# Modulation weights on buffers and a queue of their own, a second norm with its affine ahead of the transposes, and three split-weight buffers

## The chip, the cores and the metric

The kernel runs on one core of a Trainium2 chip. The metric is the device time of one execution in microseconds (us). PE is TensorE (matmuls), DVE is VectorE, ACT is ScalarE, POOL is GpSimd; SP is the engine whose queue issues transfers. Names like L98 are line numbers of the program; after the change lines move by a few, and both numbers are given where it matters.

## What is computed

One layer of a diffusion block for 512 latent tokens with 256 context tokens ahead of them, width 1024, in float32:

```
sh1, sc1, ga1, sh2, sc2, ga2 = split(silu(c) @ w_mod + b_mod, 6)
hl = rmsnorm(x) * (1 + sc1) + sh1          # the context likewise, with c_ctx
p  = hl @ w_in                             # u, gate, q, k, v, output gate, scan gates, two branch gates
A  = silu(layernorm(dwconv(u * sigmoid(gate)))) @ w_conv_out            # y_conv
h  = bidirectional mLSTM(q, k, v), 4 heads of 512                       # context first, then latents
B  = (headnorm(h) * sigmoid(output gate)) @ w_m_out                     # y_m
x  = x + ga1 * ((sigmoid(gA) * A + sigmoid(gB) * B) @ w_out)            # x1
x  = x + ga2 * (relu((rmsnorm(x) * (1 + sc2) + sh2) @ w1) ** 2 @ w2)    # FFN, 4096 wide
out = rmsnorm(x)
```

The six modulation vectors are the columns of w_mod. The first two (sh1, sc1) are needed at once; the other four (ga1, sh2, sc2, ga2: channels 2 to 5 below) only after the mixer, and only for the latent tokens.

## The kernel before

All products are made in full precision from three passes of a faster matmul: each operand is split into a high part and a low part (the rest), and `mm3` (L101 to L104) adds high x high, high x low and low x high into one PSUM bank of 512 columns.

**Weights.** `wpiece` (L88) brings one piece of 512 KB (128 x 1024): a raw buffer (three of them, `wraw`), a transfer on SP's queue (L94), for w_out a multiplication by ga1 on DVE (L96), the high part by a cast on ACT (L97), the low part by a subtraction on DVE (L98). High and low parts go round in four buffers each. Activations are split the same way by `split` (L107, L108).

**Stages.** In order: the input's norm and modulation with the first feature tiles (0 to 60 us); the four heads of the mLSTM with the convolution's branch interleaved (to about 780); the end of the last head (its attention times v, `po`; its norm, L560 to L562; its transposes `th`) and the last five tiles of the branch gates (`pab`) to about 833; y_conv (w_conv_out, `pc`); y_m (w_m_out, `pym`); x1 (w_out, `pwo`, all eight PSUM banks open at once); the second norm; the FFN. In the first head the scan's gate recursions (L265 to L307) lie on DVE, beside the short convolutions (L334) and the wide one (L374).

**The late modulation.** `mod(ch, j)` (L643) fetches one 512 KB piece of w_mod's transposed columns (`wmt`, L645) and multiplies it on DVE by silu(c), spread over the partitions in `cB`, summing along the row (L646). There are 32 such pieces, four channels of eight. Their raw buffers are those of the weights, three for both, and their transfers go through SP's queue between the weights' (one also carries `hraw`, the mixer's output read back, L687). They are called from a list of small jobs (`queue`, `pump`) between the products of the gates, of y_conv and of y_m.

**The second norm.** For each of four tiles of 128 tokens, the last w_out products (the pieces from NP1 = 4 on) are added, then the residual (L783), the mean of squares on ACT, and the reciprocal root on POOL (L81, L82). Then ACT scales by it (L796), PE transposes 128 x 128 blocks (L799), and the affine with (1 + sc2) and sh2, which are per partition after the transpose, is done on the way out of PSUM: per block one operation on ACT (L805, the high part) and two on DVE (L807, L809, the low part).

**What sets the order.** The program is written engine-free; a scheduler orders each engine's instructions, and every engine and the SP queue then run their own list strictly in order. A tile from a pool of n buffers has to wait for the reader of the tile n before it.

Of the kernel before, what the change touches and what calls it, by code (L numbers as in the profile page):

```python
# [8 lines left out]
F32 = mybir.dt.float32  # L9
# [15 lines left out]
NS = 6                      # feature tiles computed while the input's norm comes in  # L25
NX = 3                      # and these while the context's comes in
# [7 lines left out]
# columns of the packed per-partition constants  # L34
# [13 lines left out]
def block(ctx, tc, a, out):  # L48
# [9 lines left out]
    # ------------------------------------------------------------ constants  # L58
# [25 lines left out]
    # ------------------------------------------------- weights in two parts  # L84
# [56 lines left out]
    with ExitStack() as hs:  # L141
# [3 lines left out]
        # ================================================ adaLN of the input  # L145
# [88 lines left out]
        # the context's part of the input, a tile between products  # L234
# [12 lines left out]
        # ============================================ heads of the mixer, GLU  # L247
# [133 lines left out]
        # statistics of the LayerNorm, about the mean of the first channels  # L381
# [188 lines left out]
        # first head: what needs only latent tokens goes first  # L570
# [34 lines left out]
    # ============================ branch gates, both branches, output, FFN  # L605
    with ExitStack() as fs:
        # over the heads' pools that are done first
        ma = fs.enter_context(tc.tile_pool(name="ma", bufs=7))
# [5 lines left out]
        def m4(shape, dt, nm, early=False):  # L614
            return (ma if early else mp).tile(shape, dt, tag="m", name=nm, bufs=7 if early else 9)
# [15 lines left out]
        cv = []  # L631
        for j in range(KT):
            if j % 2 == 0:
                c_ = m4([P, 2, T], F32, "cv", True)
            nc.sync.dma_start(out=c_[:, j % 2, :], in_=cdr[j])
            cv.append(c_[:, j % 2, :])

        # the other modulation columns (latent only)
# [4 lines left out]
        def mod(ch, j):  # L643
            raw = wraw("wmt")
            nc.sync.dma_start(out=raw, in_=a["wmt"][ch, j])  # L645
            nc.vector.scalar_tensor_tensor(out=raw, in0=raw, scalar=1.0, in1=cB, op0=ALU.mult, op1=ALU.mult,  # L646
                                           accum_out=modc[:, ch, j:j + 1])
# [33 lines left out]
        # the mixer's output in the transposed layout, read back in two parts  # L681
        hm_ = []

        def hmload(k):
            t_ = m4([P, 2, T], F32R, "hmT", k < 4) if k < KT else h6([P, 2, T], F32R, "hmT")
            raw = wraw("hraw")
            nc.sync.dma_start(out=raw[:, :T], in_=hd[k])  # L687
            split(t_[:, 0, :], t_[:, 1, :], raw[:, :T])
            hm_.append(t_)
# [6 lines left out]
        def row(ch, nm):  # L696
            r_ = m1p.tile([P, D], F32, tag="r2", name=nm)
            pr = bank("pr")
            nc.tensor.transpose(pr[0:KT, 0:P], modc[:, ch, :], ident)
            t_ = t2("rowt", P)  # L700
            nc.scalar.copy(out=t_[0:KT, :], in_=pr[0:KT, 0:P])
            rd = dr.tile([KT, P], F32, name=f"rowd{ch}")
# [4 lines left out]
        # y_conv, then y_m  # L707
# [7 lines left out]
        ga1 = row(2, "ga1")  # L715
        yT = []
        ws = []
        for j in range(KT):
            pc = bank("pym")
            for s in range(2):  # L720
                w = wpiece(a["wmo"][j, s], (KT, P))
                for k in range(KT):
                    kk = 8 * s + k
                    mm3(pc, (w[0][:, k, :], w[1][:, k, :]), (hm_[kk][:, 0, :], hm_[kk][:, 1, :]), kk == 0, kk == 15)
            if j == KT - 1:
# [4 lines left out]
            yt = m4([P, 2, T], F32R, "yT", j < 3)  # L730
            split(yt[:, 0, :], yt[:, 1, :], y_)
            yT.append(yt)
            pump(3)
        nc.vector.tensor_scalar(out=affc, in0=modc[:, 4, :], scalar1=1.0, scalar2=None, op0=ALU.add)
        nc.vector.tensor_tensor(out=affc, in0=affc, in1=ccol(O_G2, KT), op=ALU.mult)
# [20 lines left out]
        pump(99)  # L756
# [13 lines left out]
        h2T = [m4([P, 2, T], F32R, "h2T", k < 4) for k in range(KT)]  # L770
        for t in range(NT):
# [19 lines left out]
            xhs, pts = [], []  # L791
            for hf in range(2):
                pt = bank_a("pt2")
                pts.append(pt)
                xh = t2("xh")
                nc.scalar.activation(out=xh, in_=x1[t][:, hf * 512:(hf + 1) * 512], func=AF.Copy, scale=sq[:, 3:4])  # L796
# [187 lines left out]
```

## Time and profile before

| | |
|---|---|
| Time, median of 3 runs | 1386.22 us (1385.11 to 1386.37) |
| The profiled execution: span | 1384.5 us, that is 1.7 below the median |
| Input's norm, 0 to 60 us | PE busy 45.94 |
| First head, 110 to 230 | PE busy 114.61 of 120 |
| 230 to 742 | PE busy 512 of 512 |
| End of the last head and gates, 742 to 831 | PE busy 83.67 of 89 |
| y_conv and y_m, 831 to 963.6 | PE busy 132.6 of 132.6 |
| x1 and second norm, 963.6 to 1022 | PE busy 48.74 of 58.4 |
| FFN, 1022 to 1360 | PE busy 335.43 of 338 |

The profile lists for each engine its busy time; the waits name the instruction that waited, what ended the wait, and total, count and longest. In a timeline row stand the start, the duration, the engine, the line, the operation, what it writes and reads, and in square brackets the idle time just before it with what ended that. In a row of the windows stand, after the stretch and its length, the busy time and instructions of PE, PE's weight load, DVE, ACT and POOL, then the clock that TensorE was granted (1.00 is full), the busy share of the DMA engines, and GB/s.

### The profile page before, as it was taken

Reading aid. Unit: us, or ns where it says so; the run is one execution under the profiler, and the core shown is the slowest. Engines: PE = TensorE matmul, PEld = TensorE weight load, DVE = VectorE, ACT = ScalarE, POOL = GpSimd, SP = SyncE. Lnnn points to the kernel's source line nnn. Section 1 sums busy time; section 2 is a strip of 40 time slices with the busy share of each in tenths; the row PEclk is TensorE's granted clock in tenths of the full one; section 3 lists DMA queues with packets and bytes.
Section 4 is the critical chain, followed back from the end, with each engine's and each line's share of the span. In section 5 each row is a group of like instructions: output and inputs, shape, how many; then the busy total and the mean of one; then the engine's idle time right before and its main releaser. Section 6 shows DMA issues by size and latency. Waiting matters only on the chain.

```text
span 1384.5 us, 18697 instructions
## 1 busy us (share of the span) xinstructions
PE 1339.5 (97%) x7224; PEld 1155.2 (83%) x7224; DVE 951.5 (69%) x1532; ACT 608.3 (44%) x970; POOL 55.3 (4%) x199
## 2 busy tenths in 40 slices
PE   6999999999999999999999899999789999999997
PEld 4788889888998889988899778888678888888886
DVE  6799988489574895849995564666676554545454
ACT  4547554346443464434634373222376323433232
POOL 1000100000000000000000000000010000000001
PEclk9999999999999999999999999999899999999999
DMA  8783233223322233222324475776723223432211
GB/s 317 267 327 97 87 102 111 62 66 98 117 79 63 75 93 112 80 62 76 101 87 143 154 235 168 245 235 191 229 90 122 92 69 99 122 107 92 63 60 61
DMA packets 64604, 174.89 MB, mean 126 GB/s; under 512 B 6514, under 2 KB 18946, under 8 KB 64516
## 3 DMA queue, kind: packets, MB, share of 16 engines
q1 hardware_dynamic: 64516, 173.71, 39.4%
q8 instruction: 56, 0.92, 0.3%
q14 instruction: 32, 0.26, 0.1%
HBM read 161.68 MB, written 12.00 MB: 125 GB/s over the span
## 4 chain that ended last, share of the span: by engine, by line
PE 73%; DMA 10%; DVE 9%; ACT 4%; issue 3%; POOL 1%; SPq 0%; POOLq 0%; ACTq 0%; DVEq 0%
PE pf L103 8%; PE pf L102 8%; PE pf L104 8%; DMA wmt<-in_wmt 4%; PE pv L102 2%; PE pv L104 2%; PE pv L103 2%; PE pg L104 2%; PE pg L102 2%; PE pg L103 2%; PE pq L104 2%; PE pq L102 2%; PE pq L103 2%; DVE wlo L98 2%; PE p L104 2%
## 5 line engine op out<-in xcount | busy, mean ns | idle before, releaser
L97 ACT CAST whi<-wraw 128x1024 fp32r<-128x1024 f32 (+1 forms) x159 | 164.9, 1039 | 218.2 <-PE pf L103 43.7
L98 DVE TENSOR_TENSOR wlo<-wraw,whi 128x1024 fp32r<-128x1024 f32 (+1 forms) x159 | 191.8, 1208 | 91.6 <-ACT whi L97 90.8
L374 DVE SCALAR_TENSOR_TENSOR ca<-up,col,ca 128x512 f32<-128x512 f32 x240 | 179.5, 748 | 4.7 <-ACT ca L372 0.9
L334 DVE SCALAR_TENSOR_TENSOR cacc<-craw,col,cacc 128x512 f32<-128x512 f32 (+1 forms) x128 | 110.9, 881 | 0.1
L102 PE MATMUL pv<-whi,hT 128*128 128x256 f32 x384 | 109.3, 285 | 0.0
L104 PE MATMUL pv<-whi,hT 128*128 128x256 f32 x384 | 108.6, 283 | 0.0
L103 PE MATMUL pv<-wlo,hT 128*128 128x256 f32 x384 | 108.6, 283 | 0.0
L102 PE MATMUL pf<-w2h,fT 128*128 128x512 f32 x256 | 99.6, 389 | 0.0
L103 PE MATMUL pf<-w2l,fT 128*128 128x512 f32 x256 | 99.6, 389 | 0.0
L104 PE MATMUL pf<-w2h,fT 128*128 128x512 f32 x256 | 99.6, 389 | 0.0
L858 ACT CAST w2h<-w2raw 128x1024 fp32r<-128x1024 f32 x32 | 32.2, 1050 | 133.8 <-PE pf L104 111.5
L878 DVE TENSOR_TENSOR x<-pf,x 128x512 f32<-128x512 f32 x64 | 44.1, 689 | 63.8 <-PE pf L104 63.8
L102 PE MATMUL pf<-h2T,whi 128*128 128x512 f32 x224 | 87.1, 389 | 0.0
L103 PE MATMUL pf<-h2T,whi 128*128 128x512 f32 x224 | 87.1, 389 | 0.0
L104 PE MATMUL pf<-h2T,wlo 128*128 128x512 f32 x224 | 87.1, 389 | 0.0
L103 PE MATMUL p<-wlo,hT 128*128 128x256 f32 x256 | 73.2, 286 | 3.3 <-DVE wlo L98 3.3
L103 PEld LDWEIGHTS pv<-wlo,hT 128*128 128x128 f32 x384 | 73.7, 192 | 0.2 <-issue 0.2
L102 PEld LDWEIGHTS pv<-whi,hT 128*128 128x128 f32 x384 | 73.7, 192 | 0.2 <-DVE up L356 0.2
L104 PEld LDWEIGHTS pv<-whi,hT 128*128 128x128 f32 x384 | 73.7, 192 | 0.0
L102 PE MATMUL p<-whi,hT 128*128 128x256 f32 x256 | 73.0, 285 | 0.0
L104 PE MATMUL p<-whi,hT 128*128 128x256 f32 x256 | 73.0, 285 | 0.0
L856 DVE TENSOR_TENSOR w2raw<-w2raw,ga 128x1024 f32<-128x1024 f32 x32 | 39.0, 1225 | 47.9 <-DMA w2raw<-in_w 46.7
(350 smaller groups left out, 3463.7 us busy)
## 6 DMA issues: line engine op xcount, KB each, us to landing
wm<-in_wmt SPq DMA_DIRECT2D x32, 512.0 KB, 5.7
wraw<-in_wqk SPq DMA_DIRECT2D x32, 512.0 KB, 3.6
wmt<-in_wmt SPq DMA_DIRECT2D x32, 512.0 KB, 4.2
wraw<-in_w SPq DMA_DIRECT2D x32, 512.0 KB, 4.6
w2raw<-in_w SPq DMA_DIRECT2D x32, 512.0 KB, 3.5
wraw<-in_wglu SPq DMA_DIRECT2D x16, 512.0 KB, 4.4
wraw<-in_wp SPq DMA_DIRECT2D x16, 512.0 KB, 3.5
wraw<-in_wv SPq DMA_DIRECT2D x16, 512.0 KB, 3.6
```

Of the source, the lines that this page charges most:

```text
L97: nc.scalar.copy(out=hi[:, s], in_=raw[:, s])
L98: nc.vector.tensor_tensor(out=lo[:, s], in0=raw[:, s], in1=hi[:, s].bitcast(F32), op=ALU.subtract)
L102: mm(dst, lhsT=l[0], rhs=r[0], start=start, stop=False)
L103: mm(dst, lhsT=l[0], rhs=r[1], start=False, stop=False)
L104: mm(dst, lhsT=l[1], rhs=r[0], start=False, stop=stop)
L334: nc.vector.scalar_tensor_tensor(out=acc[:, :n], in0=raw[:, d:d + n], scalar=ccol(wc + d), in1=acc[:, :n], op0=ALU.mult, op1=ALU.add)
L374: nc.vector.scalar_tensor_tensor(out=accv, in0=up[:, :, d:d + 64], scalar=w_, in1=accv, op0=ALU.mult, op1=ALU.add)
L856: nc.vector.tensor_tensor(out=raw, in0=raw, in1=ga2, op=ALU.mult)
L858: nc.scalar.copy(out=hi, in_=raw)
L878: nc.vector.tensor_tensor(out=x1[t][:, nn], in0=pf, in1=x1[t][:, nn], op=ALU.add)
```

## The change

1. **Late modulation.** The 32 pieces get two buffers of their own ("wm"), and their transfers are issued by POOL (L651) instead of SP. `mod()` multiplies the piece that came longest ago (L658) and then fetches the next but one; two are fetched where the code stands. In program order one `mod()` stands after each tile of the branch gates, after each product of y_conv and after each half of y_m.
2. **Second norm.** (1 + sc2) times the norm's gain, and sh2, are transposed, written to DRAM and read back spread over all partitions (`aff2`, `sh2`). DVE applies reciprocal root and aff2 in one operation (L812), adds sh2 (L814), then PE transposes (L817), and one `split` per half tile (128 x 4 x 128) makes the high and low part.
3. **Buffers.** High and low parts of weights: three buffers each, not four. The convolved branch `cv`, the first half of the read-back mixer output and the norm's output `h2T` share one tile of 32 KB per partition ("big"); `hraw` gets buffers of its own pool. NP1 is 5 instead of 4.

```diff
-    wp = ctx.enter_context(tc.tile_pool(name="wp", bufs=4))
+    wp = ctx.enter_context(tc.tile_pool(name="wp", bufs=3))
...
-        def mod(ch, j):
-            raw = wraw("wmt")
-            nc.sync.dma_start(out=raw, in_=a["wmt"][ch, j])
+        mods = deque((ch, j) for ch in (2, 3, 4, 5) for j in range(KT))
+        mraw = deque()
+
+        def modfetch():
+            if mods:
+                ch, j = mods.popleft()
+                raw = wp.tile([P, D], F32, tag="wm", name="wmt", bufs=2)
+                nc.gpsimd.dma_start(out=raw, in_=a["wmt"][ch, j])
+                mraw.append((ch, j, raw))
+
+        def mod():
+            if not mraw:
+                return
+            ch, j, raw = mraw.popleft()
             nc.vector.scalar_tensor_tensor(out=raw, in0=raw, scalar=1.0, in1=cB, op0=ALU.mult, op1=ALU.mult,
                                            accum_out=modc[:, ch, j:j + 1])
...
+            modfetch()
+        modfetch()
+        modfetch()
...
-        for j in range(KT):
-            queue.append(lambda j=j: mod(2, j))
         for i in range(NS + NX + 2, 16):
             ab_tile(i)
-            pump(2)
-        pump(8)
+            mod()
...
-            raw = wraw("hraw")
-            nc.sync.dma_start(out=raw[:, :T], in_=hd[k])
+            raw = t2("hraw")
+            nc.sync.dma_start(out=raw, in_=hd[k])
...
-        for ch in (3, 4, 5):
-            for j in range(KT):
-                queue.append(lambda ch=ch, j=j: mod(ch, j))
...
+        aff2 = row(affc, h6([P, D], F32, "aff2"))
+        sh2 = row(modc[:, 3, :], h6([P, D], F32, "sh2"))
         po = [(bank_a if i < 4 else bank)("pwo") for i in range(8)]
-        NP1 = 4
+        NP1 = 5
...
-                nc.scalar.activation(out=xh, in_=x1[t][:, hf * 512:(hf + 1) * 512], func=AF.Copy, scale=sq[:, 3:4])
+                nc.vector.scalar_tensor_tensor(out=xh, in0=x1[t][:, hh], scalar=sq[:, 3:4], in1=aff2[:, hh],
+                                               op0=ALU.mult, op1=ALU.mult)
+                nc.vector.tensor_tensor(out=xh, in0=xh, in1=sh2[:, hh], op=ALU.add)
...
-                nc.scalar.activation(out=h2T[kk][:, 0, tt], in_=ps_, func=AF.Identity,
-                                     scale=affc[:, kk:kk + 1], bias=modc[:, 3, kk:kk + 1])
-                nc.vector.tensor_scalar(out=xh[:, ks], in0=ps_, scalar1=affc[:, kk:kk + 1],
-                                        scalar2=modc[:, 3, kk:kk + 1], op0=ALU.mult, op1=ALU.add)
-                nc.vector.tensor_tensor(out=h2T[kk][:, 1, tt], in0=xh[:, ks], in1=h2T[kk][:, 0, tt].bitcast(F32),
-                                        op=ALU.subtract)
+                ptv = pt.rearrange("p (k t) -> p k t", k=4)
+                kk = slice(4 * hf, 4 * hf + 4)
+                split(h2T[:, 0, kk, tt], h2T[:, 1, kk, tt], ptv)
```

What the scheduler makes of it, at four places. POOL's list from the last head's masks (L489) to its norm (L77, L78 are the reciprocal root of one token tile), before:

```order
L489 AFFINE_SELECT E1_7135<-E1_7135 128x128
L77 TENSOR_SCALAR sq_7560<-sq_7560 128x1
L78 TENSOR_TENSOR sq_7560<-sq_7560,nhalf_75 128x1
L77 TENSOR_SCALAR sq_7585<-sq_7585 128x1
L78 TENSOR_TENSOR sq_7585<-sq_7585,nhalf_75 128x1
L77 TENSOR_SCALAR sq_7621<-sq_7621 128x1
```

and after, from the last two of the sixteen fetches that now stand between the masks and the first reciprocal root:

```order
L651 DMA wmt_8408<-in_wmt 128x1024
L651 DMA wmt_8443<-in_wmt 128x1024
L77 TENSOR_SCALAR sq_7560<-sq_7560 128x1
L78 TENSOR_TENSOR sq_7560<-sq_7560,nhalf_75 128x1
L77 TENSOR_SCALAR sq_7585<-sq_7585 128x1
L78 TENSOR_TENSOR sq_7585<-sq_7585,nhalf_75 128x1
L651 DMA wmt_8481<-in_wmt 128x1024
L77 TENSOR_SCALAR sq_7621<-sq_7621 128x1
L651 DMA wmt_8515<-in_wmt 128x1024
```

Each of these fetches waits for the DVE multiplication two pieces before it, and the norm's operations stand behind them.

DVE's list around the reciprocal for the convolution's LayerNorm (L410) and the mixer's output (`hm`, L562), before:

```order
L646 SCALAR_TENSOR_TENSOR wmt_7925,modc_79<-wmt_7925,cB_7722 128x1024
L649 TENSOR_TENSOR modc_79<-modc_79,col_66 128x8
L98 TENSOR_TENSOR wlo_7854<-wraw_7852,whi_7853 128x1024
L108 TENSOR_TENSOR vlo_7178<-pv_7500,vhi_7177 128x256
L98 TENSOR_TENSOR wlo_7892<-wraw_7890,whi_7891 128x1024
L407 SCALAR_TENSOR_TENSOR lns2_536<-ps2_7528,sq_7532 128x512
L408 TENSOR_SCALAR lns2_536<-lns2_536 128x512
L410 RECIPROCAL lns2_536<-lns2_536 128x512
L562 SCALAR_TENSOR_TENSOR hm_7559<-po_7540,sq_7560,sg_6592 128x512
```

and after:

```order
L658 SCALAR_TENSOR_TENSOR wmt_8283,modc_79<-wmt_8283,cB_7719 128x1024
L98 TENSOR_TENSOR wlo_7849<-wraw_7847,whi_7848 128x1024
L407 SCALAR_TENSOR_TENSOR lns2_536<-ps2_7528,sq_7532 128x512
L658 SCALAR_TENSOR_TENSOR wmt_8328,modc_79<-wmt_8328,cB_7719 128x1024
L408 TENSOR_SCALAR lns2_536<-lns2_536 128x512
L658 SCALAR_TENSOR_TENSOR wmt_8370,modc_79<-wmt_8370,cB_7719 128x1024
L661 TENSOR_TENSOR modc_79<-modc_79,col_66 128x8
L410 RECIPROCAL lns2_536<-lns2_536 128x512
L562 SCALAR_TENSOR_TENSOR hm_7559<-po_7540,sq_7560,sg_6592 128x512
```

The piece wmt_8370 is the sixteenth (the second channel's last), where before the eighth (wmt_7925) was the last ahead of the reciprocal. After the hm operations, six more pieces stand ahead of the convolution's LayerNorm (cv).

DVE's list in the first head, at the low part of the fourth k tile's weights (wlo_1371), before:

```order
L271 SCALAR_TENSOR_TENSOR L_1123<-Gs_1112 64x768
L98 TENSOR_TENSOR wlo_1371<-wraw_1369,whi_1370 128x1024
L374 SCALAR_TENSOR_TENSOR ca_620<-up_537,col_66,ca_620 128x512 x3
L274 SCALAR_TENSOR_TENSOR L_1123<-Gs_1112,L_1123 64x768
L374 SCALAR_TENSOR_TENSOR ca_620<-up_537,col_66,ca_620 128x512
```

and after, where another piece (wlo_1299) stands in that place and wlo_1371 comes after the scans (L285) and the k tiles' convolutions:

```order
L299 TENSOR_TENSOR Z_1145<-Fr_1130,Mx_1132 32x512
...
L334 SCALAR_TENSOR_TENSOR cacc_1160<-craw_1159,col_66,cacc_1160 128x770
L334 SCALAR_TENSOR_TENSOR cacc_1232<-craw_1231,col_66,cacc_1232 128x770
L98 TENSOR_TENSOR wlo_1371<-wraw_1369,whi_1370 128x1024
L307 COPY zm_81<-pz_1441 128x512
L98 TENSOR_TENSOR wlo_1463<-wraw_1461,whi_1462 128x1024
```

In the x1 stage, what stands on DVE ahead of the product that frees the eighth bank (sig15 from pym), before:

```order
L646 SCALAR_TENSOR_TENSOR wmt_8942,modc_79<-wmt_8942,cB_7722 128x1024
L108 TENSOR_TENSOR yT_8844<-sig14_7763,yT_8844 128x512
L649 TENSOR_TENSOR modc_79<-modc_79,col_66 128x8
L96 TENSOR_TENSOR wraw_9012<-wraw_9012,ga1_8321 128x1024
L96 TENSOR_TENSOR wraw_9043<-wraw_9043,ga1_8321 128x1024
L98 TENSOR_TENSOR wlo_9014<-wraw_9012,whi_9013 128x1024
L96 TENSOR_TENSOR wraw_9074<-wraw_9074,ga1_8321 128x1024
L728 TENSOR_TENSOR sig15_7764<-pym_8856,sig15_7764 128x512
```

and after:

```order
L108 TENSOR_TENSOR yT_8838<-sig14_7764,yT_8838 128x512
L98 TENSOR_TENSOR wlo_8919<-wraw_8917,whi_8918 128x1024
L96 TENSOR_TENSOR wraw_9043<-wraw_9043,ga1_8330 128x1024
L742 TENSOR_TENSOR sig15_7765<-pym_8846,sig15_7765 128x512
L743 TENSOR_TENSOR sig15_7765<-sig15_7765,sig7_7757 128x512
```

The last multiplication of a modulation piece (before: wmt_8942) no longer stands here, and of the three scalings of w_out pieces one is left ahead of the product.

More of the change, by code (lines that the diff above doesn't have):

```diff
@@ L612, in block, with big, m4 @@
         m3p = fs.enter_context(tc.tile_pool(name="m3p", bufs=1))
-        def m4(shape, dt, nm, early=False):
-            return (ma if early else mp).tile(shape, dt, tag="m", name=nm, bufs=7 if early else 9)
+        def big(shape, dt, nm):
+            return ma.tile(shape, dt, tag="big", name=nm)
+        def m4(shape, dt, nm):
+            return mp.tile(shape, dt, tag="m", name=nm, bufs=8)
         def s2(nm, dt=F32):
@@ L630, in block @@
             lnr.append(r_)
-        cv = []
+        cvb = big([P, KT, T], F32, "cv")
+        cv = [cvb[:, j, :] for j in range(KT)]
         for j in range(KT):
[L633 to L636, printed above, removed]
+            nc.sync.dma_start(out=cv[j], in_=cdr[j])
         cB = m3p.tile([P, D], F32, tag="r1", name="cB")
@@ L684, in hmload, with row @@
         def hmload(k):
-            t_ = m4([P, 2, T], F32R, "hmT", k < 4) if k < KT else h6([P, 2, T], F32R, "hmT")
-            raw = wraw("hraw")
-            nc.sync.dma_start(out=raw[:, :T], in_=hd[k])
-            split(t_[:, 0, :], t_[:, 1, :], raw[:, :T])
-            hm_.append(t_)
+            if k == 0:
+                hb = big([P, KT, 2, T], F32R, "hmT")
+                hm_.extend(hb[:, i, :, :] for i in range(KT))
+            if k >= KT:
+                hm_.append(h6([P, 2, T], F32R, "hmT"))
+            raw = t2("hraw")
+            nc.sync.dma_start(out=raw, in_=hd[k])
+            split(hm_[k][:, 0, :], hm_[k][:, 1, :], raw)
         for k in range(16):
             queue.append(lambda k=k: hmload(k))
-        for ch in (3, 4, 5):
-            for j in range(KT):
-                queue.append(lambda ch=ch, j=j: mod(ch, j))
-        def row(ch, nm):
-            r_ = m1p.tile([P, D], F32, tag="r2", name=nm)
+        def row(src, r_):
             pr = bank("pr")
-            nc.tensor.transpose(pr[0:KT, 0:P], modc[:, ch, :], ident)
+            nc.tensor.transpose(pr[0:KT, 0:P], src, ident)
             t_ = t2("rowt", P)
             nc.scalar.copy(out=t_[0:KT, :], in_=pr[0:KT, 0:P])
-            rd = dr.tile([KT, P], F32, name=f"rowd{ch}")
+            rd = dr.tile([KT, P], F32, name="rowd")
             nc.sync.dma_start(out=rd, in_=t_[0:KT, :])
@@ L714, in block @@
             pump(2)
-        ga1 = row(2, "ga1")
+            mod()
+        ga1 = row(modc[:, 2, :], m1p.tile([P, D], F32, tag="r2", name="ga1"))
         yT = []
@@ L724, in block @@
                     mm3(pc, (w[0][:, k, :], w[1][:, k, :]), (hm_[kk][:, 0, :], hm_[kk][:, 1, :]), kk == 0, kk == 15)
+                if s == 0:
+                    mod()
             if j == KT - 1:
@@ L755, in block @@
                             k == 0, False)
-        pump(99)
+        while mraw:
+            mod()
         def w1first(i):
@@ L769, in block @@
         w1 = [w1first(i) for i in range(4)]
-        h2T = [m4([P, 2, T], F32R, "h2T", k < 4) for k in range(KT)]
+        h2T = big([P, 2, KT, T], F32R, "h2T")
         for t in range(NT):
@@ L790, in block @@
             rstd2(sq)
-            xhs, pts = [], []
             for hf in range(2):
+                hh = slice(hf * 512, (hf + 1) * 512)
+                xh = t2("xh")
+                nc.vector.scalar_tensor_tensor(out=xh, in0=x1[t][:, hh], scalar=sq[:, 3:4], in1=aff2[:, hh],
+                                               op0=ALU.mult, op1=ALU.mult)
+                nc.vector.tensor_tensor(out=xh, in0=xh, in1=sh2[:, hh], op=ALU.add)
                 pt = bank_a("pt2")
-                pts.append(pt)
-                xh = t2("xh")
-                nc.scalar.activation(out=xh, in_=x1[t][:, hf * 512:(hf + 1) * 512], func=AF.Copy, scale=sq[:, 3:4])
                 for k in range(4):
-                    kk = 4 * hf + k
                     nc.tensor.transpose(pt[:, k * P:(k + 1) * P], xh[:, k * P:(k + 1) * P], ident)
-                xhs.append(xh)
-            for kk in range(KT):
-                ks = slice((kk % 4) * P, (kk % 4 + 1) * P)
-                ps_ = pts[kk // 4][:, ks]
-                xh = xhs[kk // 4]
-                nc.scalar.activation(out=h2T[kk][:, 0, tt], in_=ps_, func=AF.Identity,
-                                     scale=affc[:, kk:kk + 1], bias=modc[:, 3, kk:kk + 1])
-                nc.vector.tensor_scalar(out=xh[:, ks], in0=ps_, scalar1=affc[:, kk:kk + 1],
-                                        scalar2=modc[:, 3, kk:kk + 1], op0=ALU.mult, op1=ALU.add)
-                nc.vector.tensor_tensor(out=h2T[kk][:, 1, tt], in0=xh[:, ks], in1=h2T[kk][:, 0, tt].bitcast(F32),
-                                        op=ALU.subtract)
+                ptv = pt.rearrange("p (k t) -> p k t", k=4)
+                kk = slice(4 * hf, 4 * hf + 4)
+                split(h2T[:, 0, kk, tt], h2T[:, 1, kk, tt], ptv)
         NG = 8
-        ga2 = row(5, "ga2")
+        ga2 = row(modc[:, 5, :], m1p.tile([P, D], F32, tag="r2", name="ga2"))
         fg = m3p.tile([P, D], F32, tag="r1", name="fg")
@@ L845, in ff1 @@
                 nc.scalar.activation(out=rl, in_=rl, func=AF.Square)
-                ft = h6([P, 2, T], F32R, "fT") if g % 2 == 0 else m4([P, 2, T], F32R, "fT", i < 3)
+                ft = h6([P, 2, T], F32R, "fT") if g % 2 == 0 else m4([P, 2, T], F32R, "fT")
                 split(ft[:, 0, :], ft[:, 1, :], rl)
```

17 lines of the change are left out of this document (9 added, 8 removed).

## The prediction

> **What bounds the kernel now.** I read the page's engine shares and its DMA issues first, then the waits of PE (TensorE's matmuls), then windows where PE is not full, then the timeline there.
>
> ```profile
> PE 1339.5 (97%) x7224; PEld 1155.2 (83%) x7224; DVE 951.5 (69%) x1532; ACT 608.3 (44%) x970; POOL 55.3 (4%) x199
> ...
> q1 hardware_dynamic: 64516, 173.71, 39.4%
> ...
> wm<-in_wmt SPq DMA_DIRECT2D x32, 512.0 KB, 5.7
> ...
> wmt<-in_wmt SPq DMA_DIRECT2D x32, 512.0 KB, 4.2
> ...
> w2raw<-in_w SPq DMA_DIRECT2D x32, 512.0 KB, 3.5
> ```
>
> PE is busy 97% of the span of 1384.5 us, so 45 us at most can come from filling its gaps; the matmuls stay as they are. A modulation column's 512 KB takes 4.2 us from issue to landing (median), and all of them go through SP's hardware queue: the page has no row of a transfer that POOL issues.
>
> ```profile
> PE pwo L102 <- DVE sig L728: 8.6, 1, 8.6
> PE pt L207 <- DVE xt L181: 7.4, 4, 3.5
> PE th L548 <- DVE hm L562: 3.7, 2, 1.9
> PE pt L799 <- ACT xh L796: 3.7, 4, 2.4
> ...
> PE p L103 <- DVE wlo L98: 3.3, 1, 3.3
> ```
>
> The columns are total us, times, longest. Two of these waits are what the change reaches for: one of 8.6 us where the x1 product opens its eighth bank, and four of 3.7 us together ahead of the second norm's transposes. The other three lie in stages that the change touches sideways: the startup (pt L207), the first head (p L103), the last head's end (th).
>
> **Part 1, the wait at x1 goes.** DVE, SP and PE around it:
>
> ```profile
> 967.89 1.22 DVE L646 SCALAR_TENSOR_TENSOR wmt<-wmt,cB 128x1024 f32<-128x1024 f32 x1
> ...
> 969.72 1.22 DVE L96 TENSOR_TENSOR wraw<-wraw,ga 128x1024 f32<-128x1024 f32 x1
> 971.88 1.22 DVE L96 TENSOR_TENSOR wraw<-wraw,ga 128x1024 f32<-128x1024 f32 x1 [0.94 <-DMA wraw<-in_wo]
> ...
> 975.20 1.23 DVE L96 TENSOR_TENSOR wraw<-wraw,ga 128x1024 f32<-128x1024 f32 x1 [0.96 <-DMA wraw<-in_wo]
> 976.34 0.69 DVE L728 TENSOR_TENSOR sig<-pym,sig 128x512 f32<-128x512 f32 x1
> ```
> ```profile
> 957.31 5.26 SPq L645 DMA_DIRECT2D wmt<-in_wmt  x3
> 965.67 3.81 SPq L94 DMA_DIRECT2D wraw<-in_wo  x3
> ```
> ```profile
> 977.08 0.80 PE L102 MATMUL pwo<-whi,yT 128*128 128x512 f32 x1 [8.57 <-DVE sig L728]
> 977.67 0.63 PE L103 MATMUL pwo<-wlo,yT 128*128 128x512 f32 x1
> 978.10 0.63 PE L104 MATMUL pwo<-whi,yT 128*128 128x512 f32 x1
> ...
> 981.48 0.39 PE L103 MATMUL pwo<-wlo,yT 128*128 128x512 f32 x1
> 981.71 0.39 PE L104 MATMUL pwo<-whi,yT 128*128 128x512 f32 x1
> ```
> ```profile
> 970.00:980.00 10.00, 2.92 (x7) 2.37 (x8) 7.56 (x8) 3.75 (x4) 0.00 (x0) 0.56 0.95 340
> 980.00:990.00 10.00, 10.00 (x43) 8.22 (x42) 5.62 (x5) 1.05 (x1) 0.00 (x0) 0.93 0.51 168
> ```
>
> The last three modulation columns hold SP's queue until 965.67, so three w_out pieces are issued late; DVE, in order, stands on their scaling (L96) before it reaches L728, which frees the bank. After the stall the granted clock is 0.56 and then 0.93 (the third column from the right), and some ten matmuls come 0.43 us apart instead of 0.23: about 2.0 us more. In the new order all columns are multiplied before y_m, and L742 (the old L728) has a single scaling of an early piece ahead of it. So -8.6 - 2.0 = **-10.6 us**. What is late next is the transfer of the w_out pieces, now with x, aff2 and sh2 beside them; the products of one piece over eight banks take 24 x 0.23 = 5.5 us, longer than a landing, so I charge nothing.
>
> **Part 2, the second norm.** ACT's scaling before the transposes becomes two DVE operations of 128x512, after them, a cast on ACT and a subtraction on DVE of 512 columns a half replace eight operations of ACT and sixteen of DVE on 128 columns. NP1 = 5 leaves 3 pieces of products (3 x 5.5 = 16.4 us of PE) for four norms to hide behind instead of 4 pieces. By the 0.69 us of L728's shape a norm's DVE part is 4 x 0.69 plus two subtractions, some 4.1 us, as long as one token tile's quarter of those products. I take the 3.7 us as gone and give back 0.8: **-2.9 us** (bounds -3.7 and +2). Both parts together -13.5.
>
> **Part 3, startup.** The first two columns are now fetched by POOL within the first 3 us.
>
> ```profile
> 5.00:10.00 5.00, 2.10 (x3) 0.33 (x1) 1.61 (x4) 3.29 (x5) 0.75 (x2) 1.00 1.01 397
> 10.00:15.00 5.00, 1.42 (x3) 0.55 (x3) 3.36 (x6) 3.33 (x7) 4.09 (x6) 1.00 1.03 414
> ```
>
> The DMA engines are full there (share 1.01 and 1.03) and PE waits for x. 1.05 MB more at 400 GB/s is 2.6 us if it all goes ahead of x, nothing if it falls between. I take **+2.0** (0 to 3).
>
> **Part 4, three split buffers.** The piece for the fourth k tile of the first head:
>
> ```profile
> 128.56 1.21 DVE L98 TENSOR_TENSOR wlo<-wraw,whi 128x1024 fp32r<-128x1024 f32 x1
> ...
> 150.68 7.54 DVE L334 SCALAR_TENSOR_TENSOR cacc<-craw,col,cacc 128x770 f32<-128x770 f32 x8
> 158.13 3.49 DVE L98 TENSOR_TENSOR wlo<-wraw,whi 128x1024 fp32r<-128x1024 f32 x3
> ```
> ```profile
> 146.68 0.28 PE L102 MATMUL pk<-hT,whi 128*128 128x256 f32 x1
> ```
> ```profile
> 150.00:160.00 10.00, 6.73 (x35) 5.29 (x33) 9.97 (x12) 2.61 (x5) 0.00 (x0) 0.94 0.09 20
> ...
> 170.00:180.00 10.00, 9.25 (x78) 9.05 (x76) 9.50 (x12) 9.95 (x18) 1.54 (x5) 1.00 0.19 53
> ...
> 190.00:200.00 10.00, 8.84 (x63) 7.86 (x62) 8.00 (x28) 4.78 (x9) 0.93 (x4) 1.00 0.48 149
> ```
>
> Before, its low part is made at 128.56 and PE starts on the tile at 146.68. With three buffers it must wait for the piece two before to be used up, and the new DVE order puts it behind the scans and the eight L334 operations. One low part fewer lies ahead, so DVE reaches it at 158.1 - 1.2 = 156.9 and ends it at 158.1. PE has 1.5 us of other work, so it stands about 10 us instead of 3.3: +6.6. Afterwards DVE is no later than before, so part of the 2.1 us that PE still idles from 170 to 200 (0.75 + 1.16, and a little between) is swallowed: **+4.5** (0 to 7). In heads 1 to 3 every second piece of a pair loses its lead in the same way; PE was full there, DVE was not. No row prices it; I take **+1.5** (0 to 5).
>
> **Part 5, the end of the last head, the term that decides.**
>
> ```profile
> 750.14 1.23 DVE L646 SCALAR_TENSOR_TENSOR wmt<-wmt,cB 128x1024 f32<-128x1024 f32 x1 [2.77 <-issue]
> ...
> 783.85 1.23 DVE L646 SCALAR_TENSOR_TENSOR wmt<-wmt,cB 128x1024 f32<-128x1024 f32 x1 [2.98 <-DMA wmt<-in_wmt]
> ...
> 789.74 3.35 DVE L410 RECIPROCAL lns<-lns 128x512 f32<-128x512 f32 x1 [0.79 <-ACT lns L409]
> 793.01 1.31 DVE L562 SCALAR_TENSOR_TENSOR hm<-po,sq,sg 128x512 f32<-128x512 f32 x2
> ```
> ```profile
> 790.37 0.19 POOL L77 TENSOR_SCALAR sq<-sq 128x1 f32<-128x1 f32 x1 [63.57 <-ACT hm L560]
> ```
> ```profile
> 793.72 0.66 PE L548 MATMUL th<-ident,hm 128*128 128x128 f32 x4 [1.83 <-DVE hm L562]
> ...
> 808.09 0.66 PE L548 MATMUL th<-ident,hm 128*128 128x128 f32 x4 [1.85 <-DVE hm L562]
> ```
>
> Before, eight columns are multiplied here, from 750.14 to 785; after, 22 are, sixteen of them ahead of the reciprocal on DVE, and sixteen fetches stand on POOL's queue ahead of the rstd (L77) of the last head's first token tile. With two buffers they go in pairs: a fetch is issued when the multiplication two before is done. With L from issue to landing, a pair takes L + 1.35 us (1.23 and the semaphore's way). The third starts at 751.4 + L, the fifteenth six pairs later, the sixteenth ends 2.5 us after that starts: 751.4 + L + 6(L + 1.35) + 2.5 = 762.0 + 7L. The reciprocal was free to start at 789.74: the delay is 7L - 27.7, if that is above zero. For L = 3.5 nothing, for 4.2 1.7 us, for 5.7 12.2 us. DVE's vlo and wlo behind the columns cost about 1.5 us more, and PE's later wait for hm (1.85 at 808.09) is swallowed. L is not in the trace, and its bounds are the rows above: 3.5 and 5.7. I take 4.7, half a microsecond over the row of this same transfer, since it starts on an idle queue but shares with the pair's other half: 5.2 + 1.5 - 1.8 = **+5.0** (-1 to +12).
>
> The Trainium skill, "DMA: Bandwidth & Descriptors", section "Anatomy of one DMA - SWDGE (gpsimd) path", fits such a transfer by 2.0 us plus its bytes over 436 GB/s, an estimate of 3.2 us for 512 KB; by that the term is 0 and the sum falls to the first rival's.
>
> **The sum.** -13.5 + 2.0 + 4.5 + 1.5 + 5.0 = -0.5 us. The profiled execution's span is 1384.5, 1.7 below the median of 1386.2, and I let that 1.7 stand: **1385.7 us**.
>
> **Rivals.** (a) POOL's transfers are as quick as the quickest row, L = 3.5: part 5 is 0 and the sum -5.5: 1380.7; if the first head also swallows its stall, 1376. For it: POOL is idle 96% of the time and its queue has nothing else. Against: the same 512 KB through SP's queue take 4.2.
>
> (b) The change ends slower: POOL writes and starts these transfers later than SP's queue does, and L is 6. Sixteen columns then end at 804, the reciprocal, all hm, the cv operations and the two low parts for the last gate tiles (behind cv on DVE) shift: 14.3 + 1.5 - 1.8 + 4 for the cv chain = 18, sum +12.5: 1398.7. It decides from L = 5.2, where the sum passes +2.8. For it: sixteen fetches in a row, each waiting on DVE, ahead of L77, and DVE in order behind each landing. Against: no row of 512 KB reaches 6 as a median, even in the full startup (5.7).
>
> The Trainium skill, "SBUF - State Buffer", section "SBUF: two separate sides", says that a transfer issued from GpSimd can starve while DVE runs in a mode that holds both ports, because its descriptors cannot be written; no run here shows it yet, and it would be this rival's cause.
>
> (c) The change does not do what it says: the eighth bank still opens late because w_out's loads now queue with x and the two broadcast rows. Price 8.6, 1394. Against: DVE's order has one scaling ahead of L742.
>
> **How the numbers follow.** The forecast's case (L from 4.3 to 5.2) gets 0.42, (a) 0.30, (b) 0.20, (c) 0.08. The 1385.7 is the first one's. A measurement of this kernel can tell about 0.2%, 2.8 us, from no change. The forecast's own range is 1379 to 1392: faster by more than 0.2% in 0.28 of it, slower in 0.32. (a) is faster in 0.85 and the same in 0.15; (b) is slower; (c) is slower in 0.05 of its 0.08, the same in 0.02, faster in 0.01. Faster 0.12 + 0.25 + 0.01 = 0.38, same 0.17 + 0.04 + 0.02 = 0.23, slower 0.13 + 0.20 + 0.06 = 0.39. The range takes in nearly all of (a) and (b) up to L = 6.3: 1374 to 1402.
>
> **What would show it.** Right: the wait pwo on sig gone and none over 1 us in its place; transposes pt2 without waits; the issue row of wmt on POOL near 4.7; a wait of p on wlo of about 10 us near 150; th's first wait near 7 us. Wrong: a POOL row under 4.2 or over 5.3, PE full from 145 to 160, or a new wait at x1, in the norm or in y_conv.

## The result and the profile after

The changed kernel takes 1396.93 us (median of 4 runs, 1394.28 to 1398.27) against 1386.3; the ratio is 1.0072, 95% interval 1.0057 to 1.0087. It is slower, inside the stated range, and 11.2 us above the forecast's own time; the chances had slower (0.39) and faster (0.38) about level. The profiled execution is the longest of the four; its span is 1396.5 us, 12.0 more than the one before, where the medians differ by 10.6.

The rows of the page that were missing before: POOL's queue, and the columns' transfers on it.

```profile
PE 1345.0 (96%) x7226; PEld 1160.0 (83%) x7226; DVE 948.4 (68%) x1492; ACT 597.8 (43%) x940; POOL 71.1 (5%) x231
...
q0 software_dynamic: 4608, 16.78, 3.9%
...
wmt<-in_wmt POOLq DMA_DIRECT2D x32, 512.0 KB, 4.7
```

The 512 KB take 4.7 us from issue to landing, the median of all 32, and the value that the prediction chose. The waits of PE in the changed kernel:

```profile
PE pt L207 <- DVE xt L181: 9.4, 4, 3.4
PE pk L104 <- DVE wlo L98: 6.8, 1, 6.8
PE th L548 <- DVE hm L562: 6.6, 1, 6.6
PE pv L103 <- DVE wlo L98: 5.5, 4, 3.5
PE pab L104 <- DVE wlo L98: 5.1, 1, 5.1
...
PE pz L305 <- issue: 1.9, 1, 1.9
PE pt L817 <- DVE xh L814: 1.0, 2, 0.7
```

The 8.6 us of pwo are gone, and of the 3.7 us at the second norm 1.0 is left. In their place stand a wait in the first head (pk), and three in one stage, the end of the last head: v's products (pv), the mixer's output (th) and the branch gates (pab). Where the time went, by the starts of the same matmuls in the two timelines (us; "heads" runs from the first head's gate products to the last head's v products, "last head's end" from there to the first y_conv product, "x1 on" from the first w_out product to the last matmul):

| | startup | heads | last head's end | y_conv, y_m | x1 on |
|---|---|---|---|---|---|
| before | 62.2 | 682.5 | 88.1 | 130.7 | 412.9 |
| changed | 65.3 | 689.7 | 102.9 | 130.9 | 399.5 |
| difference | +3.0 | +7.2 | +14.8 | +0.1 | -13.4 |
| predicted | +2.0 | +6.0 | +5.0 | 0 | -13.5 |

Four of five terms came out within 1.2 us. The last head's end is off by 9.8, nearly all of the miss. The x1 stage and the norm in one window of the changed kernel (PE 47.69 of 48 us, clock 1.00):

```profile
988.00:1036.00 48.00, 47.69 (x222) 38.48 (x222) 31.29 (x41) 19.54 (x35) 2.03 (x5) 1.00 0.52 167
```

DVE at the end of the last head; L658 is a column's multiplication, the rows are the 12th, 15th and 16th column, the reciprocal, hm, and the low part for the last gate tile but one:

```profile
794.32 1.23 DVE L658 SCALAR_TENSOR_TENSOR wmt<-wmt,cB 128x1024 f32<-128x1024 f32 x1 [3.45 <-DMA wmt<-in_wmt]
...
805.53 1.23 DVE L658 SCALAR_TENSOR_TENSOR wmt<-wmt,cB 128x1024 f32<-128x1024 f32 x1 [2.75 <-DMA wmt<-in_wmt]
...
808.29 1.23 DVE L658 SCALAR_TENSOR_TENSOR wmt<-wmt,cB 128x1024 f32<-128x1024 f32 x1 [1.19 <-DMA wmt<-in_wmt]
...
809.64 3.35 DVE L410 RECIPROCAL lns<-lns 128x512 f32<-128x512 f32 x1
812.90 1.31 DVE L562 SCALAR_TENSOR_TENSOR hm<-po,sq,sg 128x512 f32<-128x512 f32 x2
...
844.39 1.22 DVE L98 TENSOR_TENSOR wlo<-wraw,whi 128x1024 fp32r<-128x1024 f32 x1
```

and PE, at the three places where it waits for them:

```profile
777.45 0.58 PE L103 MATMUL pv<-wlo,hT 128*128 128x256 f32 x1 [3.46 <-DVE wlo L98]
...
813.61 1.12 PE L548 MATMUL th<-ident,hm 128*128 128x128 f32 x4 [6.59 <-DVE hm L562]
...
845.66 0.80 PE L104 MATMUL pab<-hT,wlo 128*128 128x512 f32 x1 [5.05 <-DVE wlo L98]
846.25 0.63 PE L102 MATMUL pab<-hT,whi 128*128 128x512 f32 x1
846.68 0.63 PE L103 MATMUL pab<-hT,whi 128*128 128x512 f32 x1
```

At the first place DVE sits idle for a column's transfer while a low part, whose high part ACT has made, stands behind it. At the second, hm stands behind the reciprocal, and the reciprocal behind the sixteenth column; the first two roots on POOL, which hm needs as well, are ready before DVE reaches hm, at 811.26 and 812.18. At the third place DVE does not wait for a column: the low part stands behind fifteen of the sixteen operations on cv, and DVE waits there for cv's own transfer, which SP issues behind the fourth of the stores of the mixer's output (`hd`):

```profile
832.23 0.37 SPq L553 DMA_DIRECT2D hd<-st  x1
832.64 3.01 SPq L637 DMA_DIRECT2D cv<-cdr  x5
```
```profile
838.89 1.36 DVE L669 TENSOR_TENSOR cv<-cv,lnr 128x512 f32<-128x512 f32 x2 [3.33 <-DMA cv<-cdr]
```

Before the change SP issued cv's eight transfers behind the first store and the second. The scheduler moved them: three stand behind the third now, five behind the fourth.

```profile
797.06 0.39 SPq L553 DMA_DIRECT2D hd<-st  x1
797.54 1.95 SPq L635 DMA_DIRECT2D cv<-cdr  x4
```

Each stall also costs PE slow matmuls after it (0.43 us apart here, not 0.23).

### The profile page after: what moved, and what is told of

Its sections match the earlier page's. It is cut to its first block, busy times and chain, and to the rows that moved or that the text cites. A ratio compares the mean times of both kernels' runs of the same rounds, so it can differ in the third digit from the quotient of the medians.

```text
span 1396.5 us, 18647 instructions
## 1 busy us (share of the span) xinstructions
PE 1345.0 (96%) x7226; PEld 1160.0 (83%) x7226; DVE 948.4 (68%) x1492; ACT 597.8 (43%) x940; POOL 71.1 (5%) x231
```

## The experiments

The theory that went in: the 14.8 us come from where the columns stand on DVE, 22 of them ahead of hm and cv ("placement"). Rival A: POOL's queue is what costs. Rival B: three split buffers do it. All times have the kernel before beside them on the same chip (1386.3 to 1387.5 us). For each kernel the table at the end of this section has the same stages as above, each from the one profiled execution.

**Columns on SP's queue.**

```diff
-                nc.gpsimd.dma_start(out=raw, in_=a["wmt"][ch, j])
+                nc.sync.dma_start(out=raw, in_=a["wmt"][ch, j])
```

> The changed kernel with the modulation columns fetched by SP's queue instead of POOL's; buffers, program order and DVE's order (sixteen columns ahead of the reciprocal, six more ahead of cv) stay. Placement theory (the 14.7 us lost between the last head's v products and y_conv come from 22 columns standing on DVE ahead of low parts, hm and cv): the loss stays at 11 to 18 us; the startup's 3.0 us go, since SP issues the first two fetches later than POOL did; 1391 to 1398 us. Rival A (POOL's software queue is what costs): the loss falls to 5 or less and the time to 1381 to 1387. Rival B (three split buffers are what costs there): like the placement theory, 1391 to 1398.

1385.3 us, ratio 0.9996 (0.9983 to 1.0009). The last head's end loses 2.4 us instead of 14.8: placement alone falls, and rival A has the number that it gave. But the queue is not all that differs. The scheduler also put the low part for the last gate tile but one behind three operations on cv and not behind fifteen, and cv's transfers behind the second store and the third (the last two behind the fourth). PE's wait of 5.1 us for that low part is 0.5 here, and which part of the 12.4 us is the queue's this run alone cannot tell. PE's waits in that stage:

```profile
PE pv L103 <- DVE wlo L98: 2.5, 1, 2.5
PE th L548 <- DVE hm L562: 2.0, 1, 2.0
PE pab L102 <- ACT sig L682: 0.3, 1, 0.3
```

and on DVE the first and the sixteenth column, the reciprocal and that low part:

```profile
759.97 1.22 DVE L658 SCALAR_TENSOR_TENSOR wmt<-wmt,cB 128x1024 f32<-128x1024 f32 x1 [3.54 <-issue]
...
801.83 1.23 DVE L658 SCALAR_TENSOR_TENSOR wmt<-wmt,cB 128x1024 f32<-128x1024 f32 x1 [2.22 <-DMA wmt<-in_wmt]
802.99 3.35 DVE L410 RECIPROCAL lns<-lns 128x512 f32<-128x512 f32 x1
...
824.16 1.22 DVE L98 TENSOR_TENSOR wlo<-wraw,whi 128x1024 fp32r<-128x1024 f32 x1
```

The same sixteen columns still stand ahead of the reciprocal, but take 41.9 us from the first to the sixteenth instead of the changed kernel's 47.3 (760.99 to 808.29). Over the whole run DVE waits for columns nearly as long as in the changed kernel, 21.8 us in 17 waits against 23.7 in 16; what differs is where.

**Three split buffers in the kernel before.**

```diff
-    wp = ctx.enter_context(tc.tile_pool(name="wp", bufs=4))
+    wp = ctx.enter_context(tc.tile_pool(name="wp", bufs=3))
```

> The kernel before with three split-weight buffers instead of four and nothing else. Placement theory: only the first head (4.4 us) and heads 1 to 3 (2.8 us) get longer, the last head's end by 0 to 2; the x1 wait of 8.6 stays; 1392 to 1396 us. Rival B (three buffers cause the last head's loss): the end of the last head grows by 8 to 14 as well, 1400 to 1408. Rival A: as the placement theory.

1397.52 us, ratio 1.0090 (1.0058 to 1.0121); the median is 1.5 above what was expected. The heads get 8.0 us longer, the last head's end gets no longer (-1.6): rival B falls. Not expected: the x1 wait is 2.6 us and not 8.6, while the second norm's grows from 3.7 to 6.4 and x1 on is 1.3 longer; and 3.1 us in y_m.

```profile
PE pk L104 <- DVE wlo L98: 7.0, 1, 7.0
...
PE pym L104 <- DVE wlo L98: 1.8, 3, 1.3
```

**Columns behind cv.** The multiplication is ordered on DVE behind the last LayerNorm operation (`tc.issue_after` sets order on one engine, no wait):

```diff
-            nc.vector.scalar_tensor_tensor(out=raw, in0=raw, scalar=1.0, in1=cB, op0=ALU.mult, op1=ALU.mult,
-                                           accum_out=modc[:, ch, j:j + 1])
+            with tc.issue_after(cvlast.ins):
+                nc.vector.scalar_tensor_tensor(out=raw, in0=raw, scalar=1.0, in1=cB, op0=ALU.mult, op1=ALU.mult,
+                                               accum_out=modc[:, ch, j:j + 1])
```

> The changed kernel with each column's multiplication ordered on DVE behind the last of the LayerNorm operations on cv; POOL fetches, three buffers and the new norm stay. Placement theory: the loss at the last head's end falls from 14.7 to 0 to 4 us, the x1 wait stays gone; 1381 to 1387 us. Rival B: the waits of pv and pab for low parts (3.5 and 5.1 us with the slow matmuls behind them) stay; 1390 to 1394. Rival A says nothing different from the placement theory here, since nobody waits for a late column.

1391.81 us, ratio 1.0048 (1.0026 to 1.0069). The last head's end is now 5.4 us shorter than before the change, but y_conv and y_m lose 11.9 us. The loss moved with the columns:

```profile
PE pym L104 <- DVE wlo L98: 4.6, 2, 4.0
...
PE pc L104 <- DVE wlo L98: 3.2, 1, 3.2
```
```profile
933.18 1.22 DVE L659 SCALAR_TENSOR_TENSOR wmt<-wmt,cB 128x1024 f32<-128x1024 f32 x1 [3.56 <-DMA wmt<-in_wmt]
```

The scheduler again puts columns as early as it may, DVE stands on their transfers (3.56 us at this one), and low parts wait behind. That nobody waits for a late column was wrong: the low part behind it does.

**The same, first fetches late.**

```diff
-        modfetch()
-        modfetch()
+        with tc.issue_after(pw[-1].ins):
+            modfetch()
+            modfetch()
```

> As the run with late columns, and the first two fetches issued by POOL only behind the last head's last reciprocal root instead of in the first 3 us. If the 1 MB ahead of x is what costs the startup 3.0 us: 2.5 to 3.5 us less than the run with late columns, 1378 to 1384 us, with the start of the first feature products back at 18.5 us. If the startup's loss is something else: the same as that run.

1392.26 us, ratio 1.0045 (1.0028 to 1.0062): no shorter as a whole. The startup does go back (62.8 us instead of 64.9, first feature products at 18.61 instead of 20.98), so the two fetches are what cost it; y_conv and y_m give it back, with 5.0 us more than the run above; DVE waits 24.3 us for columns, 20.1 there. The profiled execution is the longest of its seven, 3.1 us above their median, so that the 5.0 is not sure to the microsecond.

**Columns paced, on POOL's and on SP's queue.** A second theory: what costs is DVE standing in order on columns whose transfer has not landed; the queue sets how long it stands. So each multiplication is ordered behind the low part of the piece beside which it stands in the program, one per piece:

```diff
+        lows.append(nc.vector.tensor_tensor(out=lo[:, s], in0=raw[:, s], in1=hi[:, s].bitcast(F32), op=ALU.subtract))
...
+            with tc.issue_after(lows[-1].ins):
+                nc.vector.scalar_tensor_tensor(out=raw, in0=raw, scalar=1.0, in1=cB, op0=ALU.mult, op1=ALU.mult,
+                                               accum_out=modc[:, ch, j:j + 1])
```

> The changed kernel with each column's multiplication ordered on DVE behind the low part of the weight piece beside which it stands in the program, so that columns come one per piece (some 5.5 us apart) and not as early as the scheduler puts them; POOL fetches, three buffers, new norm stay. Theory 2 (the loss is DVE standing in order on columns whose transfers have not landed, with low parts, hm and cv behind them; the queue only sets how long): last head's end, y_conv and y_m together lose 0 to 3 us instead of 14.7, startup 3.0 and heads 7.2 stay, back part -13: 1382 to 1387 us. Rival A (a transfer on POOL's queue costs by itself, wherever the column stands): 5 us or more stay lost, 1389 to 1396.

> The same pacing with the columns fetched by SP's queue; DVE's order is the same up to a few places. Theory 2: only the startup's 3.0 us less than the paced run on POOL's queue, 1379 to 1384 us. Rival A: 8 us or more less than that run.

1382.88 us on POOL's queue, ratio 0.9979 (0.9969 to 0.9990), and 1380.22 on SP's, 0.9961 (0.9948 to 0.9974). Both times are inside theory 2's numbers; the last head's end takes 83.5 and 83.2 us, y_conv and y_m 130.9 in both. Rival A falls in its turn: between the two runs stand 2.6 us in the startup and 1.0 in x1 on. One number of theory 2 was missed: x1 on is 9.8 and 10.8 us shorter than before the change, not 13. Three columns now stand on DVE in the x1 stage, and the second norm's transposes wait 3.1 and 2.0 us where the changed kernel's wait 1.0. Over the whole POOL run the idle time before columns is

```profile
  DMA wmt<-in_wmt: 2.7, 3
...
DMA to landing us min/median/max: 4.1/5.0/10.1
```

where the changed kernel's is 23.7 us in 16 waits. The landings are no faster, 5.0 us; DVE just does not stand there while they are under way.

**Pacing and four split buffers.** To make room, columns go through the weights' three raw buffers again:

```diff
-    wp = ctx.enter_context(tc.tile_pool(name="wp", bufs=3))
+    wp = ctx.enter_context(tc.tile_pool(name="wp", bufs=4))
...
-                raw = wp.tile([P, D], F32, tag="wm", name="wmt", bufs=2)
+                raw = wraw("wmt")
```

> Paced columns on SP's queue through the weights' raw buffers as before the change, and four split-weight buffers; the new norm and the program order of the change stay. If three buffers cost the 7 us of heads 1 to 4 and the pacing costs nothing: 1386.4 - 13 + 0 to 4, so 1373 to 1378 us. If the shared raw buffers bring a wait back (at x1 or in y_m): 1378 to 1385.

1371.63 us, ratio 0.9903 (0.9888 to 0.9919): the fastest of all, 14.7 below the kernel before and 1.4 below the range that was given. The heads are back at 682.7 us; the shared buffers bring no wait back that shows, and x1 on stays at 402.1. The longest waits of PE:

```profile
PE pt L209 <- DVE xt L183: 7.4, 4, 3.6
PE pcr L166 <- DMA cL<-in_c: 3.6, 1, 3.6
PE p L105 <- DVE wlo L100: 3.3, 1, 3.3
```

**The kernel before, its jobs earlier.**

```diff
-            pump(2)
+            pump(3)
```

> The kernel before with three small jobs after each product of y_conv instead of two, so that its columns are all done before y_m ends; nothing else. If the x1 wait comes from the last columns on SP's queue and on DVE, 7 to 11 us go: 1375 to 1380 us. If other work makes that wait (w_out's transfers and scaling alone): less than 3 us go, 1383 to 1387.

1385.53 us, ratio 0.9997 (0.9982 to 1.0012), no change that can be told as a whole; by its time alone it would speak for other work as the cause of the x1 wait. The stages say otherwise. In its profiled execution (2.7 us below the median) x1 on takes 402.6 us, 10.3 less: the last columns do make that wait, and it was sized well (10.6). But y_conv and y_m give back 7.2 us, in the same way: SP issues a weight's transfer behind three columns', and ACT and then PE wait for it.

```profile
872.61 1.04 ACT L97 CAST whi<-wraw 128x1024 fp32r<-128x1024 f32 x1 [8.43 <-DMA wraw<-in_wco]
```
```profile
873.70 0.50 PE L102 MATMUL pc<-act,whi 128*128 128x512 f32 x1 [2.85 <-ACT whi L97]
```

**The old norm in the fastest kernel.** NP1 is 4 again, aff2 and sh2 go, and the affine stands after the transposes:

```diff
-                nc.vector.scalar_tensor_tensor(out=xh, in0=x1[t][:, hh], scalar=sq[:, 3:4], in1=aff2[:, hh],
-                                               op0=ALU.mult, op1=ALU.mult)
-                nc.vector.tensor_tensor(out=xh, in0=xh, in1=sh2[:, hh], op=ALU.add)
...
+                nc.scalar.activation(out=xh, in_=x1[t][:, hf * 512:(hf + 1) * 512], func=AF.Copy, scale=sq[:, 3:4])
```

> The paced kernel with four split buffers (1371.6 us) with the norm as before the change (affine after the transposes, NP1 4, no aff2 and sh2). If the new norm is worth what the prediction took: 2 to 4 us longer, 1373.5 to 1375.5. If the norm's idle time would have gone anyway with the x1 wait: the same within 1 us.

1375.82 us, ratio 0.9919 (0.9898 to 0.9940), a little over the range that was given. The time is 4.2 us above the kernel with the new norm, but that one ran beside a kernel before of 1386.28 and this one beside 1387.48: the ratios differ by 0.0016, or 2.2 us, and their intervals overlap. The stages are firmer: x1 on is 4.3 us longer, of which 2.9 are the wait ahead of the transposes, here with the new norm and then with the old:

```profile
PE pt L818 <- DVE xh L815: 1.8, 4, 0.5
```
```profile
PE pt L816 <- ACT xh L813: 4.7, 4, 1.9
```

**Sixteen columns on one queue, sixteen on the other.**

```diff
-                nc.gpsimd.dma_start(out=raw, in_=a["wmt"][ch, j])
+                (nc.gpsimd if ch < 4 else nc.sync).dma_start(out=raw, in_=a["wmt"][ch, j])
```

> The changed kernel with the first sixteen columns on POOL's queue and the last sixteen on SP's; in the order DVE gets, the sixteen still stand ahead of the reciprocal, but the low part of the last gate tile but one stands behind one cv operation and not behind all. If the queue's landing time sets the waits at th (5 us) and the order behind cv the wait at pab (5 us): from the v products to y_conv 7 to 9 us are lost instead of 14.7, th's wait stays 5 to 7 us, pab's goes; 1388 to 1391 us. If the landing on POOL causes both: 12 us or more lost, 1393 or more. If the order causes both: 2 to 4 us lost, 1384 to 1386.

> The other way round: the first sixteen columns on SP's queue, the last sixteen on POOL's, the same place for that low part. If the landing sets th's wait: it is 2 us as with all columns on SP's queue, 2 to 4 us lost to y_conv, 1384 to 1388 us. If POOL's queue costs in the later columns too: 1388 or more.

POOL first: 1390.81 us, ratio 1.0025 (1.0010 to 1.0040); 7.9 us lost in the last head's end, th's wait 5.4, no wait of pab for a low part. That is the first of its three cases. SP first: 1390.26 us, 1.0024 (1.0012 to 1.0037); 8.7 us lost, not the 2 to 4 of its first case; the time is that of its second, POOL's queue costing in the later columns too. Its th waits 2.3 us, much as with SP alone (2.0), but a gate tile's products wait 4.5 us for a sigmoid behind cv's on ACT, and cv is late:

```profile
827.85 0.69 DVE L669 TENSOR_TENSOR cv<-cv,lnr 128x512 f32<-128x512 f32 x1 [3.62 <-DMA cv<-cdr]
```

DVE waits there for cv's own transfer and not for a column. The loss against the kernel before, split at the gates' first product of this stage, and how long after that product DVE starts the last operation on cv (8.6 us in the kernel before):

| us | up to the gates | from the gates on | last operation on cv |
|---|---|---|---|
| changed kernel | +9.8 | +5.0 | 22.5 |
| columns on SP | +3.7 | -1.3 | 16.7 |
| POOL first, then SP | +7.3 | +0.5 | 18.6 |
| SP first, then POOL | +2.7 | +6.0 | 25.2 |

The first loss goes with the queue of the first sixteen columns. The second goes with how late cv is done, and not with the place of the low part, which with SP first stands behind a single operation on cv. In both kernels that lose there, DVE waits over 3 us for a transfer of cv that SP issues behind the third or the fourth store. But with the columns behind cv those transfers stand behind the same two stores and nothing is lost in the gates, so their place alone does not do it, and what makes cv late stays open.

| us | startup | heads | last head's end | y_conv, y_m | x1 on |
|---|---|---|---|---|---|
| columns on SP | 62.2 | 691.6 | 90.5 | 130.9 | 399.8 |
| before, three buffers | 63.1 | 690.5 | 86.6 | 133.8 | 414.2 |
| columns behind cv | 64.9 | 691.5 | 82.7 | 142.6 | 399.4 |
| the same, fetched late | 62.8 | 690.8 | 84.5 | 147.6 | 399.6 |
| paced, POOL | 65.0 | 691.5 | 83.5 | 130.9 | 403.1 |
| paced, SP | 62.4 | 691.5 | 83.2 | 130.9 | 402.1 |
| paced, four buffers | 60.6 | 682.7 | 83.5 | 130.8 | 402.1 |
| before, jobs earlier | 64.0 | 682.1 | 86.5 | 137.9 | 402.6 |
| paced, four buffers, old norm | 62.3 | 682.2 | 83.2 | 130.7 | 406.4 |
| POOL first, then SP | 64.9 | 691.4 | 96.0 | 130.9 | 399.8 |
| SP first, then POOL | 63.2 | 690.6 | 96.9 | 130.9 | 399.6 |

## Why the prediction was wrong

**Part 1 (-10.6) and part 2 (-2.9): right.** x1 on is 13.4 us shorter. The earlier jobs, which keep the old norm, give 10.3 by themselves; the old norm put back makes x1 on 4.3 longer in a kernel without the x1 wait.

**Part 3 (+2.0): right, a little small.** +3.0, the upper end; the late fetch takes it away. Startups of programs that begin alike differ by up to 1.8 us in the table, so the one microsecond between 2.0 and 3.0 means nothing.

**Part 4 (+6.0): right.** +7.2 in the changed kernel, +8.0 as the only edit. In the first head alone, from the gate products to the first v products, it is 4.4 us against the 4.5 worked out. That it is so near is in part luck: PE waits 1.9 us (pz) and 6.8 (pk) there, not about 10, slow matmuls follow, and all of the later 2.1 us are swallowed, not a part. It also counted one low part fewer ahead on DVE, and another piece's took that place.

**Part 5 (+5.0): the step that failed, in two of its terms.** Counted from the first v product, the gates' first products start 9.8 us late where 5.0 was summed up, and from there to y_conv another 5.0 us are lost where the sum had nothing. So the miss of 9.8 is 4.8 in the delay of the chain and 5.0 in the gates behind it, a wait that the sum left out.

First, the delay. The reciprocal starts at 809.64; with the shift of 10.2 us by which the last head begins later, that is 9.7 us late where 5.2 was worked out. 762.0 + 7L took one landing time for all pairs. Between the first and the sixteenth column it makes 43.5 us at L = 4.7; measured are 47.3. The fetches from the third to the fourteenth landed faster than that, in 4.2 us (median):

```profile
DMA to landing us min/median/max: 3.8/4.2/5.5
```

The fifteenth fetch is issued here:

```profile
797.33 0.54 POOL L651 DMA_DIRECT2D wmt<-in_wmt  x1 [0.94 <-DVE wmt L658]
```

and its column starts at 805.53, 8.2 us later; the sixteenth starts 7.0 us after its fetch. In the same microseconds SP issues weights and the LayerNorm's rows, and the DMA engines are full (share 1.00):

```profile
802.00:806.00 4.00, 4.00 (x20) 3.30 (x19) 1.25 (x3) 0.00 (x0) 0.00 (x0) 1.00 1.00 376
```

The Trainium skill, "DMA: Bandwidth & Descriptors", section "Issuing engines are not separate DMA queues", says that transfers issued by different engines run on the same DMA engines and interleave; this row, with transfers of both queues under way, agrees. That the full engines are what delayed the fifteenth is likely and not shown: with POOL first, a fifteenth fetch issued as close ahead of the same weight (797.41) has its column 4.2 us later, and there it is the sixteenth that takes 7.5. The estimate of 3.2 us for 512 KB, by the fit of the Trainium skill's same page, section "Anatomy of one DMA - SWDGE (gpsimd) path", was too short here: the median is 4.7, the least 3.8.

So L as the median of all 32 was right, in part by luck: the first five of the chain's six pairs took 29.3 us in all where 30.3 was worked out, and the last, at 9.7 in place of 6.05, made the delay. The 1.5 us for low parts and vlo were set on top; v's products lost 5.2 us, 3.46 waiting and the rest in slow matmuls, but this lies inside the 9.7, since PE then comes later to hm. That is also why th's first wait is 6.6, as forecast, behind a delay that is not.

Second, the low part behind cv was priced only under rival (b), 4 us, as a shift of the whole chain; it came with L = 4.7 as well, 5.05 us of waiting and 1.6 in the slow matmuls after it. Ahead of it DVE waits 3.33 us for cv's transfer; SP's order, which moved that transfer, is not among the orders that were read.

**The rivals.** (b) was nearest by its number (1398.7) and by its mechanism, in-order DVE behind landings. Its condition was wrong: it came at L = 4.7, not from 5.2; and its number is near by offsetting, 18 us for this stage where 14.8 came, startup and heads 2.2 too low. What was held against it was wrong too: the kernel before does have rows of 512 KB that reach 6 us as a median, in the startup, in the view of its transfers:

```profile
xt<-in_x SPq DMA_DIRECT2D x4, 512.0 KB, 7.4
...
xt<-in_ctx SPq DMA_DIRECT2D x2, 512.0 KB, 6.7
```

Its cause by the Trainium skill ("SBUF — State Buffer", section "SBUF: two separate sides"), descriptors starved by DVE, no run here shows: paced beside the same DVE work, POOL's transfers take 5.0 us, and SP's 4.6 in the 11 of 32 whose landing the trace has. (a) did not occur, nor (c), whose 0.05 for slower was added up as 0.06; that changes nothing.

**What is settled and what is not.** Shown: paced, the same columns cost the last head's end nothing on either queue; crowded, they delay the gates by 9.8 and 7.3 us with the first sixteen on POOL's queue and by 3.7 and 2.7 with them on SP's. So it is neither queue nor place alone: crowded columns make DVE's progress hang on each landing. Open: why the sixteenth column on POOL's queue comes 3.5 to 5.4 us later than on SP's. Up to the third column 0.6 to 0.7 of that are there, from the third to the thirteenth 0.3 to 1.5, and in the last three 2.6 to 3.2; POOL issues some 0.3 us after DVE is done, SP 0.1. Open too: what makes cv late, and with it the loss in the gates, where the columns stand crowded; and the 3.1 us that three buffers cost y_m in the kernel before and not in the changed one.

## What to carry to other kernels

On an in-order engine a fetched operand that nobody needs soon should be consumed at the pace at which it can land, next to work of that pace; a scheduler that places it as early as it may can turn a late landing into a wait of whatever stands behind. Price such a chain by its number of landings and by the transfers that share the DMA engines at that moment, not by one median, and ask of each instruction that the chain passes who waits for it. Compare the order of every queue before and after, that of the queue that issues transfers too. Price a buffer less by looking for the instruction that moves behind a long run on its engine: that came within 0.1 us here as a sum, and within some 1.3 us in its wait.

## What the runs showed of the hardware

The 512 KB that POOL issued took 4.7 to 5.3 us (median) from issue to landing in runs where all columns went that way; SP's took 4.4 to 4.6 with the same buffers, in the 13 and 11 of 32 transfers whose landing those traces have. POOL is busy 0.54 us with each issue. After a stall of 3.5 to 6.6 us the granted clock was 0.50, and the next 8 to 15 matmuls ran at about half speed (0.43 us apart in place of 0.23 for 512 columns), so that a stall cost PE 1.5 to 2 us more than its wait.
